# A differential softmax combined by one VectorE instruction in place of two on GpSimd, and three PSUM banks used in turn by transposes, PV products and norm statistics

## The chip, the cores and the metric

The kernel runs on one core of one Trainium2 chip. The metric is the device time of one execution in microseconds: 3506.85 us before (median of three runs, 3505.14 to 3511.03). The engines are TensorE (PE; its weight loads are PEld), VectorE (DVE), ScalarE (ACT), GpSimd (POOL) and SyncE (SP, which here only starts DMA transfers). Each works through its own instructions in the order of the program and waits at an instruction whose inputs or buffers are not ready.

## The reference

Two layers of a diffusion transformer over 128 context tokens and 1024 latent tokens with 1024 features. In each layer a normalised input is projected once to the queries, keys and values of three groups of heads: A (neighbourhood attention, 4 heads), B (windowed attention with a sink, 8 query heads) and C (differential attention, 4 heads); then an output projection with a gated residual, another normalisation and a gated MLP with a convolution over positions. The change is in C:

```
def diff_attn(q, k, v, lam, subln_g, lam_init):
    o1 = dense_attn(q[..., 0, :], k[..., 0, :], v).astype(F32)
    o2 = dense_attn(q[..., 1, :], k[..., 1, :], v).astype(F32)
    o = rmsnorm(o1 - lam * o2, subln_g) * (1.0 - lam_init)
    return o.astype(v.dtype)
```

Each of the two `dense_attn` is softmax(q k / sqrt(d)) v. For the latent tokens the keys are the 1024 latent keys and 256 cached ones, so a block of 128 queries has 128 x 1280 scores per component; the 128 context tokens see only each other.

## The kernel before, in words

Activations lie transposed, features on the 128 partitions and tokens along the free dimension, 1156 columns in three chunks of about 386. A weight matmul is made of three fp32r products of high and low parts (`gemm`, L496). A layer runs as: input projections and attention A and B, woven together after `PLAN`; attention C (`attnC`); the output projection of A and B (`outproj_part`, whose operand is read back from DRAM as `oraw` and split into `o`, L639 and L640); that of C with the normalisation; the MLP (`ffn`, `down`). In layer 0 some modulation vectors are computed between the parts of the output projection (`mod_piece`, L392); those of layer 1 come from `mod_vec` beside the MLP.

`attnC` goes head by head. It loads queries and keys (L699, L703, issued on GpSimd's queue) and the cached keys (`kc`, L705, on SyncE's queue), which GpSimd splits into the key tile (`kr`, L707, L708). There are two buffers for queries and two for keys, one for each component, so a head's loads begin when the last scores of the head before are done. Then come the context block and four pairs of query blocks. For each block and component: score matmuls (L732), a VectorE reduction that copies the scores to `P` and takes the row maximum (L734), an exponential with row sums on ScalarE (L685). With the two row sums in `ss`, VectorE takes the reciprocal of one (L741) and computes the factor that weighs the second component against the first (L742); GpSimd multiplies the second component's `P` by it (L743) and adds it to the first's (L744). The pair goes to `tpv`: 20 transposes in five groups of four (L652), each copied to SBUF by ScalarE (L654), 20 PV matmuls into one bank (L661) and two copies to `O` (L665). Half heads are rescaled (`rows_over`, L757), and after every second head `subln` normalises.

The scheduler that writes the program (`schedule_with_timeline_sim=True`) decides the order on each engine: it takes instructions in the program's order as a priority, with a cost model of its own, and fills what it takes for idle time with later work. So the output projection of A and B stands between the instructions of `attnC`.

PSUM has eight banks, given out by tag. `s` (three) holds scores, `mm` (two) matmul outputs, `tb` (two) transposes and a few others, `pv` (one) PV products. A request for a tag takes the next bank of that tag in turn and waits until the use before it has been released. Input projections go round all eight (`MM_IN`), and statistics of the normalisations take `tb`, `tb` and `pv`.

Of the kernel before, what the change touches and what calls it, by code (L numbers as in the profile page):

```python
# [11 lines left out]
ALU = mybir.AluOpType  # L12
# [23 lines left out]
FGROUP = 3  # L36
NFG = 7
XW = 1156
BANKS = {"s": 3, "tb": 2, "pv": 1, "mm": 2}
MM_FILL = ["mm"]  # L40
MM_SOLO = ["mm", "s", "s", "mm", "s"]
MM_IN = ["mm", "s", "s", "mm", "s", "tb", "tb", "pv"]
ENG = {"v": lambda nc: nc.vector, "p": lambda nc: nc.gpsimd}
FLUSH = (2, 4, 6, 7)
CG = 2
# [3 lines left out]
GATE = 3  # L49
TAGS = {"F": MM_FILL, "P": ["mm", "s", "s", "mm", "s"], "Q": MM_IN}  # L50
MV0 = 12
# [20 lines left out]
def bcast(ap, n):  # L72
    return bass.AP(tensor=ap.tensor, offset=ap.offset, ap=[list(ap.ap[0])] + n)
# [15 lines left out]
class Trunk:  # L89
# [11 lines left out]
    def bank(self, tag):  # L101
        return self.psp.tile([128, 512], F32, name=tag, bufs=BANKS[tag])

# [10 lines left out]
    def run(self):  # L114
        nc, a = self.nc, self.a
        with ExitStack() as st:
# [8 lines left out]
            x = xp.tile([128, KT, XW], F32, name="x")  # L125
# [22 lines left out]
                        st.enter_context(self.tc.issue_after(dm[3].ins))  # L148
            self.gate = dm[GATE]
            self.consts()  # L150
            stats = [self.bank(x) for x in ("tb", "tb", "pv")]
            for t in range(3):
                self.stats(np_, x, stats[t], t, range(KT))
            hp0, hs0 = self.open("h0")
# [6 lines left out]
            for l in range(self.depth):  # L161
# [5 lines left out]
                xs.close()  # L167
                self.mmtags = MM_IN
                self.O = {}
# [27 lines left out]
                x = xp.tile([128, KT, XW], F32, name="x")  # L197
# [19 lines left out]
                np_, ns = self.open("norm", "right")  # L217
                ohp, ohs = self.open("ohl")
                self.h = [None] * 3
                stats = [self.bank(x) for x in ("tb", "tb", "pv")]  # L220
                ow = [self.finO(ohp, t, {k: self.O[k][:, OCHUNK[t][0]:OCHUNK[t][1]] for k in (6, 7)}, 12) for t in range(3)]
                for ts in ((0,), (1, 2)):
                    for ob in range(KT):
                        if ob % 4 == 0:
                            whl = self.wload(a["woc"][l, ob // 4], nc.vector)
                        for t in ts:
                            c0, c1 = OCHUNK[t]
                            ps = self.mm()
# [14 lines left out]
                ms.close()  # L243
                hs1.close()
                if l + 1 < self.depth:
                    stats = [self.bank(x) for x in ("tb", "tb", "pv")]
                    self.op, os_ = self.open("O32")
                    h0n, h0s = self.open("h0")
                    np_, ns = self.open("norm")
                    self.h = [None] * 3  # L250
# [153 lines left out]
    def mod_vec(self, l, j, mp):  # L404
        nc = self.nc
        X = 512 // CG
        acc = [mp.tile([128, X], F32, name="macc", bufs=MODF[1]) for _ in range(2)]
        for k in range(8):
            raw = mp.tile([128, 512], F32, name="mraw", bufs=MODF[0])
            nc.sync.dma_start(raw, self.a["wmv"][12 * l + j - MV0, k])  # L410
            for b in range(CG):
                for v in range(2):
                    c = self.svm[:, CG * k + b, v:v + 1]
                    r = raw[:, X * b:X * b + X]
                    if k == 0 and b == 0:
                        nc.vector.tensor_scalar(acc[v], r, c, None, op0=ALU.mult)
                    else:
                        nc.vector.scalar_tensor_tensor(acc[v], r, c, acc[v], op0=ALU.mult, op1=ALU.add)
        ps = self.bank("pv")
        for i in range(4 // CG):  # L420
            for v in range(2):
                o = 2 * i + v
                nc.tensor.matmul(ps[:, o:8:8 // CG], acc[v][:, 128 * i:128 * i + 128], self.blk, start=True, stop=True)
        self.mod_end(l, j, ps)
# [219 lines left out]
    def tpv(self, ap, items, V, bufs, outs):  # L644
        nc = self.nc
        pts = []
        for g in range(0, len(items), 4):
            its = items[g:g + 4]
            n = 128 * len(its)
            t = self.tb()  # L650
            for j, it in enumerate(its):
                nc.tensor.transpose(t[:, 128 * j:128 * j + 128], it[0], self.ident)  # L652
            pt = ap.tile([128, 512], F32, name="pt", bufs=bufs)
            nc.scalar.activation(pt[:, :n], t[:, :n], AF.Copy)  # L654
            pts.append(pt)
        ps = self.bank("pv")
        left = [sum(it[2] == i for it in items) for i in range(2)]
        first = [True, True]
        for g, (_, vb, i) in enumerate(items):
            left[i] -= 1  # L660
            nc.tensor.matmul(ps[64 * i:64 * i + 64, :128], V[:, vb], pts[g // 4][:, 128 * (g % 4):128 * (g % 4) + 128],  # L661
                             start=first[i], stop=left[i] == 0)
            first[i] = False
        for dst, p0, p1, view in outs:
            nc.scalar.activation(dst, view(ps[p0:p1, :128]), AF.Copy)  # L665
# [21 lines left out]
    def attnC(self, ap):  # L687
        nc, l = self.nc, self.l
        G, qkv = GROUPS["C"], self.qkv["C"]
        lam = self.lam[l]  # L690
        O = V = None
        for h in range(4):
            blk, rw = h // 2, 64 * (h % 2)
            Q, K = [], []
            for c in range(2):
                q = ap.tile([128, W], F32R, name="q", bufs=NQ_C)
                s = qkv[G["q"][blk]][rw // 32 + c]
# [3 lines left out]
                s = qkv[G["k"][blk]][rw // 32 + c]  # L701
# [16 lines left out]
            for q0 in (None, 0, 2, 4, 6):  # L718
                Pq = []
                for i in range(1 if q0 is None else 2):  # L720
                    P2 = []
                    nm = ap.tile([128, 6], F32, name="nm", bufs=4)
                    ss = ap.tile([128, 3], F32, name="ss", bufs=4)
                    qo = C0 if q0 is None else L0 + 128 * (q0 + i)
                    P2 = [ap.tile([128, 1280], F32, name="P", bufs=NP_C) for c in range(2)]
                    parts = [(C0, 0, 128)] if q0 is None else [(L0, 0, 512), (L0 + 512, 512, 512), (L0 + 1024, 1024, 256)]
                    n = parts[-1][1] + parts[-1][2]
                    prev = [self.big] * 2
                    for u, (ko, po, w) in enumerate(parts):
                        for c in range(2):  # L730
                            s = self.sc()[:, :w]
                            nc.tensor.matmul(s, Q[c][:, qo:qo + 128], K[c][:, ko:ko + w], start=True, stop=True)  # L732
                            acc = nm[:, 3 * c + u:3 * c + u + 1]
                            nc.vector.tensor_tensor_reduce(P2[c][:, po:po + w], s, bcast(self.zero, [[0, w]]), -1.0, prev[c],  # L734
                                                           op0=ALU.add, op1=ALU.min, accum_out=acc)
                            prev[c] = acc
                    for c in range(2):
                        self.softrow(P2[c], n, prev[c], ss[:, c:c + 1])
                    r = sums[:, q0 + i:q0 + i + 1] if q0 is not None else ss[:, 2:3]
                    nc.vector.reciprocal(r, ss[:, 0:1])  # L740
                    nc.vector.reciprocal(ss[:, 1:2], ss[:, 1:2])  # L741
                    nc.vector.scalar_tensor_tensor(ss[:, 1:2], ss[:, 1:2], lam[:, 1:2], ss[:, 0:1], op0=ALU.mult, op1=ALU.mult)  # L742
                    nc.gpsimd.tensor_scalar(P2[1][:, :n], P2[1][:, :n], ss[:, 1:2], 0.0, op0=ALU.mult, op1=ALU.add)  # L743
                    nc.gpsimd.tensor_tensor(P2[0][:, :n], P2[0][:, :n], P2[1][:, :n], op=ALU.add)  # L744
                    if q0 is None:
                        nc.vector.tensor_scalar(P2[0][:, :n], P2[0][:, :n], r, None, op0=ALU.mult)
                    Pq.append(P2[0])
                if q0 is None:
                    self.tpv(ap, [(Pq[0][:, :128], 0, 0)], V, NT_C, [(O[rows, C0:C0 + SEQ], 0, 64, lambda z: z)])
                    continue  # L750
                qo = L0 + 128 * q0
                self.tpv(ap, [(Pq[i][:, 128 * k:128 * k + 128], k + 1, i) for k in range(10) for i in range(2)], V, NT_C,
                         [(O[rows, qo + 128 * i:qo + 128 * i + 128], 64 * i, 64 * i + 64, lambda z: z) for i in range(2)])
                if q0 in (2, 6):
                    R = self.rows_over(sums[:, q0 - 2:q0 + 2], 1)[rows]
                    oo = O[rows, L0 + 128 * (q0 - 2):L0 + 128 * (q0 + 2)]
                    nc.vector.tensor_tensor(oo, oo, R, op=ALU.mult)  # L757
                    if h % 2 == 1:
                        for c0, c1 in NCHUNK[:1] if q0 == 2 else NCHUNK[1:]:
                            self.subln(ap, O, c0, c1)  # L760
# [367 lines left out]
```

## Time and profile before

| what | value |
|---|---|
| time, median of three runs | 3506.85 us |
| time of the profiled execution | 3506.57 us |
| its span | 3504.8 us |
| TensorE busy | 3322.5 us (95%) |
| VectorE busy | 2043.1 us (58%) |
| ScalarE busy | 1505.4 us (43%) |
| GpSimd busy | 1213.5 us (35%) |
| instructions | 54130 |

Busy time is a share of the whole span and hides that the stages differ: TensorE is at 88 of 88 us in most stretches of the MLP, and at 70 to 87 in those of attention C. The profiler's granted clock is the share of TensorE's full 2.4 GHz; its lower level, 1.2 GHz, is 0.50. A group of instructions is named by line, engine, operation and tile, with `x` for its count, busy time and the mean of one in ns.

### The profile page before, as it was taken

What the parts mean: (1) busy time and instruction counts of PE and PEld (TensorE: products, weight loads), DVE (VectorE), ACT (ScalarE), POOL (GpSimd) and SP (SyncE); (2) the same over time, 40 slices, a digit from 0 to 9 for tenths busy, and PEclk for the clock granted to TensorE, in tenths of its full rate; (3) what the DMA queues carried; (4) which work ended last, traced back from release to release, by engine and by line L of the source; (5) the groups of instructions that cost most, each with busy time, mean ns of one, the idle gap of its engine ahead of it and who ended that gap; (6) DMA issues with size and microseconds to landing.
All of it is one profiled execution on the core that took longest, in us unless ns stands there. A gap on an engine that the chain in (4) does not pass through costs nothing. (4 is left out here: it accounts for less than half of the span.)

```text
span 3504.8 us, 54130 instructions
## 1 busy us (share of the span) xinstructions
PE 3322.5 (95%) x20398; PEld 3012.4 (86%) x20398; DVE 2043.1 (58%) x4666; ACT 1505.4 (43%) x2905; POOL 1213.5 (35%) x1252
## 2 busy tenths in 40 slices
PE   6999998897899999999999989989888999999999
PEld 4987885684699999999989878858667999999999
DVE  5355466665676765676573554567667544544445
ACT  4566575545432222222245656665564322232222
POOL 6444246645611111111154442476565111111110
PEclk9999998897899999999999999999989999999999
DMA  5764338413112222222136652363201011111112
GB/s 202 203 162 130 94 100 217 133 37 93 34 61 73 85 76 67 82 85 78 43 125 189 169 134 74 109 165 82 52 17 36 32 46 44 43 37 46 46 40 93
DMA packets 184565, 318.21 MB, mean 91 GB/s; under 512 B 58544, under 2 KB 126528, under 8 KB 183920
## 3 DMA queue, kind: packets, MB, share of 16 engines
q1 hardware_dynamic: 170320, 266.18, 24.7%
q0 software_dynamic: 13984, 48.57, 6.8%
q8 instruction: 162, 2.65, 0.3%
q14 instruction: 99, 0.81, 0.1%
HBM read 260.15 MB, written 58.73 MB: 91 GB/s over the span
## 5 line engine op out<-in xcount | busy, mean ns | idle before, releaser
L496 PE MATMUL mm<-h,whl 128*128 128x386 f32 (+2 forms) x4488 | 888.0, 345 | 9.8 <-DVE h L484 4.3
L496 PEld LDWEIGHTS mm<-h,whl 128*128 128x128 f32 x4488 | 796.4, 190 | 29.3 <-DVE h L484 5.8
L496 PE MATMUL s<-h,whl 128*128 128x386 f32 (+2 forms) x4152 | 781.9, 342 | 15.7 <-ACT h L483 10.6
L496 PEld LDWEIGHTS s<-h,whl 128*128 128x128 f32 x4152 | 740.2, 190 | 29.9 <-ACT h L483 15.3
L378 POOL TENSOR_TENSOR whl<-wraw,whl 128x1024 fp32r<-128x1024 f32 x88 | 211.5, 2403 | 1344.5 <-ACT whl L377 1258.2
L685 ACT ACTIVATE P<-P,nm 128x641 f32<-128x641 f32 (+5 forms) x360 | 345.3, 960 | 169.5 <-DVE nm L734 89.6
L377 ACT ACTIVATE whl<-wraw 128x1024 fp32r<-128x1024 f32 (+1 forms) x210 | 207.5, 988 | 450.0 <-PE s L496 255.9
L496 PE MATMUL s<-ah,whl 128*128 128x384 f32 (+1 forms) x1268 | 356.6, 341 | 1.6 <-DVE x L918 1.2
L654 ACT ACTIVATE pt<-tb 128x512 f32<-128x512 f32 (+2 forms) x456 | 237.0, 541 | 147.2 <-PE tb L652 144.1
L652 PE MATMUL tb<-ident,P 128*128 128x128 f32 x1600 | 269.8, 289 | 14.9 <-ACT pt L654 7.5
L661 PE MATMUL pv<-pt,v 128*64 128x128 f32 x3200 | 264.0, 287 | 6.6 <-ACT pt L654 2.9
L918 DVE SCALAR_TENSOR_TENSOR x<-s,m,x 128x128 f32<-128x128 f32 (+3 forms) x347 | 170.0, 514 | 153.6 <-PE s L496 153.2
L918 DVE SCALAR_TENSOR_TENSOR x<-mm,m,x 128x128 f32<-128x128 f32 (+3 forms) x357 | 175.2, 513 | 142.1 <-PE mm L496 141.7
L652 PEld LDWEIGHTS tb<-ident,P 128*128 128x128 f32 x1600 | 189.7, 145 | 72.9 <-issue 36.3
L496 PE MATMUL mm<-ah,whl 128*128 128x384 f32 (+1 forms) x844 | 244.1, 340 | 1.4 <-DVE x L918 1.4
L661 PEld LDWEIGHTS pv<-pt,v 128*64 128x64 f32 x3200 | 173.7, 138 | 83.3 <-issue 54.6
L496 PEld LDWEIGHTS s<-ah,whl 128*128 128x128 f32 x1268 | 233.6, 189 | 5.9 <-DVE x L918 1.7
L496 PE MATMUL mm<-o,whl 128*128 128x384 f32 (+1 forms) x972 | 210.4, 354 | 11.7 <-ACT o L639 6.6
L496 PE MATMUL s<-al,whl 128*128 128x384 f32 (+1 forms) x634 | 215.1, 339 | 0.0
L496 PEld LDWEIGHTS mm<-o,whl 128*128 128x128 f32 x972 | 178.2, 197 | 24.5 <-issue 7.4
L682 PE MATMUL s<-k,q 128*128 128x256 f32 (+2 forms) x816 | 178.5, 333 | 19.2 <-DMA q<-d 11.5
L744 POOL TENSOR_TENSOR P<-P 128x1280 f32<-128x1280 f32 (+1 forms) x72 | 192.2, 2671 | 4.5
(208 smaller groups left out, 4971.8 us busy)
## 6 DMA issues: line engine op xcount, KB each, us to landing
wraw<-wup SPq DMA_DIRECT2D x88, 512.0 KB
mraw<-wmod SPq DMA_DIRECT2D x48, 512.0 KB
mraw<-wmv SPq DMA_DIRECT2D x96, 256.0 KB
wraw<-wdn SPq DMA_DIRECT2D x64, 384.0 KB
k<-d POOLq DMA_DIRECT2D x80, 288.5 KB, 6.5
wraw<-win SPq DMA_DIRECT2D x36, 512.0 KB
d<-hl SPq DMA_DIRECT2D x28, 386.0 KB
q<-d POOLq DMA_DIRECT2D x32, 289.0 KB, 6.6
```

What stands on the lines that cost most here:

```text
L377: nc.scalar.activation(hl[:, 0, :n], raw[:, :n], AF.Copy)
L378: lo_eng.tensor_tensor(hl[:, 1, :n], raw[:, :n], hl[:, 0, :n].bitcast(F32), op=ALU.subtract)
L496: nc.tensor.matmul(ps, w_, r_[:, a:b], start=(i == 0), stop=(i == tot - 1))
L652: nc.tensor.transpose(t[:, 128 * j:128 * j + 128], it[0], self.ident)
L654: nc.scalar.activation(pt[:, :n], t[:, :n], AF.Copy)
L661: nc.tensor.matmul(ps[64 * i:64 * i + 64, :128], V[:, vb], pts[g // 4][:, 128 * (g % 4):128 * (g % 4) + 128], start=first[i], stop=left[i] ...
L682: nc.tensor.matmul(dst, q, view(ks[i]), start=(i == 0), stop=(i == 1))
L685: self.nc.scalar.activation(P[:, :n], P[:, :n], AF.Exp, scale=-1.0, bias=nm, accum_out=sums)
L744: nc.gpsimd.tensor_tensor(P2[0][:, :n], P2[0][:, :n], P2[1][:, :n], op=ALU.add)
L918: nc.vector.scalar_tensor_tensor(xx, ps[:, s - a:e - a], m[:, col + ob, v:v + 1], xx, op0=ALU.mult, op1=ALU.add)
```

## The change

In `attnC` the two GpSimd instructions L743 and L744 become one VectorE instruction that multiplies the second component by the factor and adds the first. The factor itself (L742) is computed by another form with the same three inputs. The bank tags become `s` (three), `tb` (three) and `mm` (two): PV products, the vectors of `mod_vec` and the third bank of the statistics are taken from `tb`, in turn with the transposes. Lines after the combine have a number smaller by one in the changed kernel.

```
-BANKS = {"s": 3, "tb": 2, "pv": 1, "mm": 2}
+BANKS = {"s": 3, "tb": 3, "mm": 2}
...
-MM_IN = ["mm", "s", "s", "mm", "s", "tb", "tb", "pv"]
+MM_IN = ["mm", "s", "s", "mm", "s", "tb", "tb", "tb"]
...
-            stats = [self.bank(x) for x in ("tb", "tb", "pv")]
+            stats = [self.bank(x) for x in ("tb", "tb", "tb")]
...
-        ps = self.bank("pv")
+        ps = self.tb()
...
-                    nc.vector.scalar_tensor_tensor(ss[:, 1:2], ss[:, 1:2], lam[:, 1:2], ss[:, 0:1], op0=ALU.mult, op1=ALU.mult)
-                    nc.gpsimd.tensor_scalar(P2[1][:, :n], P2[1][:, :n], ss[:, 1:2], 0.0, op0=ALU.mult, op1=ALU.add)
-                    nc.gpsimd.tensor_tensor(P2[0][:, :n], P2[0][:, :n], P2[1][:, :n], op=ALU.add)
+                    nc.vector.tensor_scalar(ss[:, 1:2], ss[:, 1:2], ss[:, 0:1], lam[:, 1:2], op0=ALU.mult, op1=ALU.mult)
+                    nc.vector.scalar_tensor_tensor(P2[0][:, :n], P2[1][:, :n], ss[:, 1:2], P2[0][:, :n], op0=ALU.mult, op1=ALU.add)
```

The statistics' line stands three times in `run`, the `ps` line once in `mod_vec` and once in `tpv`.

The scheduler writes a new order. On GpSimd, at the change from the first to the second head of C in layer 0, there stood before (`q<-d` and `k<-d` are the loads of queries and keys, `kr<-kc` needs the load of cached keys):

```order
L699 DMA q<-d_12_5669 32x1156 x4
L703 DMA k<-d_14_5612 64x1154 x2
L708 TENSOR_TENSOR k<-kc,kr 128x256
L640 TENSOR_TENSOR o<-oraw,o 128x384
L743 TENSOR_SCALAR P<-P,ss 128x1280
L699 DMA q<-d_12_5669 32x1156 x4
L703 DMA k<-d_14_5612 64x1154 x2
L743 TENSOR_SCALAR P<-P,ss 128x1280
L707 TENSOR_SCALAR kr<-kc,hsel 128x256
L744 TENSOR_TENSOR P<-P 128x1280
L640 TENSOR_TENSOR o<-oraw,o 128x384 x2
L744 TENSOR_TENSOR P<-P 128x1280
```

and stands now:

```order
L640 TENSOR_TENSOR o<-oraw,o 128x386 x2
L640 TENSOR_TENSOR o<-oraw,o 128x384 x4
L640 TENSOR_TENSOR o<-oraw,o 128x386 x4
L640 TENSOR_TENSOR o<-oraw,o 128x384 x2
L699 DMA q<-d_12_5669 32x1156 x4
L703 DMA k<-d_14_5612 64x1154 x2
L708 TENSOR_TENSOR k<-kc,kr 128x256
L699 DMA q<-d_12_5669 32x1156 x4
L703 DMA k<-d_14_5612 64x1154 x2
L707 TENSOR_SCALAR kr<-kc,hsel 128x256
L708 TENSOR_TENSOR k<-kc,kr 128x256
```

The combines of the last two blocks are gone from between the loads and `kr<-kc`, and twelve splits of the projection's operand now stand ahead of the loads. On TensorE at the same place there stood before (`s<-k,q 128x128` is the context block of the next head, `mm<-o,whl` the output projection):

```order
L661 MATMUL pv<-pt,v 64x128 x12
L732 MATMUL s<-k,q 128x128
L496 MATMUL mm<-o,whl 128x384 x3
L496 MATMUL mm<-o,whl 128x386 x6
L496 MATMUL mm<-o,whl 128x384 x7
L732 MATMUL s<-k,q 128x128
L732 MATMUL s<-k,q 128x512 x4
L732 MATMUL s<-k,q 128x256
L652 MATMUL tb<-ident,P 128x128 x2
L496 MATMUL mm<-o,whl 128x384 x10
L496 MATMUL mm<-o,whl 128x386 x6
L652 MATMUL tb<-ident,P 128x128 x6
```

and stands now, between the first and the second score of the context block:

```order
L652 MATMUL tb<-ident,P 128x128 x9
L496 MATMUL mm<-o,whl 128x384 x6
L496 MATMUL mm<-o,whl 128x386
L652 MATMUL tb<-ident,P 128x128 x4
L496 MATMUL mm<-o,whl 128x386 x5
L652 MATMUL tb<-ident,P 128x128 x4
L661 MATMUL tb<-pt,v 64x128 x16
L673 MATMUL tb<-ident,sums 128x128 x4
L496 MATMUL mm<-o,whl 128x384 x5
L661 MATMUL tb<-pt,v 64x128 x4
L496 MATMUL mm<-o,whl 128x384 x6
L732 MATMUL s<-k,q 128x128
```

The last pair's transposes and PV products have moved from behind the next head's scores to ahead of its second component. On TensorE at the start of the third head of C in layer 1 there stands before:

```order
L732 MATMUL s<-k,q 128x128
L732 MATMUL s<-k,q 128x512 x2
L496 MATMUL mm<-o,whl 128x386 x12
L652 MATMUL tb<-ident,P 128x128 x6
L496 MATMUL mm<-o,whl 128x384 x4
L732 MATMUL s<-k,q 128x512
L496 MATMUL mm<-o,whl 128x384 x3
L732 MATMUL s<-k,q 128x512
```

and now:

```order
L732 MATMUL s<-k,q 128x128
L732 MATMUL s<-k,q 128x512 x3
L767 MATMUL tb<-sq,ones_86 128x384
L732 MATMUL s<-k,q 128x512
L732 MATMUL s<-k,q 128x256 x2
L767 MATMUL tb<-sq,ones_86 128x386
L732 MATMUL s<-k,q 128x512 x4
L652 MATMUL tb<-ident,P 128x128
```

The output projection, whose 432 matmuls stood in the second and third head there, now stands in the first and second.

## Rows read from the trace of the kernel before

**Rows 1.** Stretches of attention C: busy time of each engine, clock, DMA share
```profile
537.00:897.00 360.00, 308.80 (x1950) 219.73 (x1950) 212.78 (x628) 186.15 (x343) 205.98 (x168) 0.87 0.40 113
...
2300.00:2610.00 310.00, 266.43 (x1780) 207.33 (x1776) 206.00 (x620) 179.80 (x338) 201.24 (x159) 0.91 0.27 72
```

**Rows 2.** Stretches by head and gap; columns: us, PE, PEld, DVE, ACT, POOL, clock, DMA
```profile
537.00:602.00 65.00, 57.98 (x387) 35.90 (x386) 47.94 (x143) 44.55 (x86) 46.63 (x50) 0.87 0.71 222
602.00:622.00 20.00, 7.95 (x25) 5.92 (x21) 3.10 (x10) 2.45 (x8) 10.75 (x9) 0.59 0.72 157
...
690.00:700.00 10.00, 4.28 (x15) 1.32 (x14) 1.85 (x2) 1.99 (x4) 5.47 (x6) 0.71 1.17 248
...
820.00:866.00 46.00, 40.77 (x252) 25.58 (x250) 37.43 (x125) 32.33 (x57) 26.75 (x15) 0.87 0.04 9
...
2300.00:2350.00 50.00, 41.40 (x303) 27.17 (x299) 39.49 (x141) 38.98 (x80) 35.74 (x32) 0.96 0.45 150
2350.00:2372.00 22.00, 15.67 (x96) 12.41 (x96) 8.62 (x27) 9.25 (x21) 18.44 (x21) 0.77 0.79 171
2372.00:2435.00 63.00, 63.00 (x447) 54.42 (x447) 49.08 (x147) 40.68 (x73) 47.78 (x37) 1.00 0.29 74
...
2450.00:2518.00 68.00, 64.27 (x422) 54.39 (x420) 50.76 (x144) 35.33 (x61) 29.17 (x16) 0.97 0.09 29
...
2535.00:2585.00 50.00, 42.91 (x273) 28.90 (x272) 39.98 (x122) 36.12 (x62) 33.35 (x19) 0.84 0.04 9
```

**Rows 3.** Groups by line and shape, 535 to 900 us: GpSimd's combine, copies of PV
```profile
L744 POOL TENSOR_TENSOR P<-P 128x1280 f32<-128x1280 f32 x32 | 94.9, 2968 | 1.9
...
L743 POOL TENSOR_SCALAR P<-P,ss 128x1280 f32<-128x1280 f32 x32 | 43.4, 1356 | 68.1 <-DVE ss L742 34.2 <-ACT pt L654 14.8 <-PE s L732 10.2
...
L665 ACT ACTIVATE O<-pv 64x128 f32<-64x128 f32 x36 | 9.8, 272 | 25.3 <-PE pv L661 25.0
```

**Rows 4.** Timeline of GpSimd at a head change; columns: start, duration, engine, instruction, wait
```profile
599.50 2.04 POOL L699 DMA_DIRECT2D q<-d  x4
...
609.68 0.48 POOL L707 TENSOR_SCALAR kr<-kc,hsel 128x256 fp32r<-128x256 f32 x1 [5.46 <-DMA kc<-kc]
...
613.81 1.97 POOL L640 TENSOR_TENSOR o<-oraw,o 128x384 fp32r<-128x384 f32 x2 [0.80 <-ACT o L639]
615.73 2.90 POOL L744 TENSOR_TENSOR P<-P 128x1280 f32<-128x1280 f32 x1
```

**Rows 5.** Timeline of TensorE: projection matmuls, weight loads of PV and transposes
```profile
713.08 3.96 PE L496 MATMUL mm<-o,whl 128*128 128x384 f32 x21
...
732.76 0.85 PEld L661 LDWEIGHTS pv<-pt,v 128*64 128x64 f32 x16 [0.17 <-issue]
...
875.98 0.64 PEld L652 LDWEIGHTS tb<-ident,P 128*128 128x128 f32 x6 [0.77 <-POOL P L744]
```

**Rows 6.** Timeline at the end of attention C, layer 0
```profile
866.97 2.90 POOL L744 TENSOR_TENSOR P<-P 128x1280 f32<-128x1280 f32 x1
867.10 1.35 ACT L685 ACTIVATE P<-P,nm 128x1280 f32<-128x1280 f32 x1
867.71 2.58 DVE L770 SCALAR_TENSOR_TENSOR O<-O,pp,oy 128x386 f32<-128x386 f32 x1
...
873.03 2.90 POOL L744 TENSOR_TENSOR P<-P 128x1280 f32<-128x1280 f32 x1
```

**Rows 7.** VectorE: line L526 (min/median/max in ns), and the reductions by shape, 535 to 900 us
```profile
L526 DVE SCALAR_TENSOR_TENSOR qg<-t,qg x78: 546/559/1080, 81.6 to 2306.8; 128x386 f32<-128x386 f32 x52, 128x384 f32<-128x384 f32 x26
...
L734 DVE CUSTOM_DVE_ANT_0 P<-s,zero,nm 128x512 f32<-128x512 f32 x64 | 46.9, 745 | 8.1 <-PE s L732 7.1
L734 DVE CUSTOM_DVE_ANT_0 P<-s,zero,nm 128x256 f32<-128x256 f32 x64 | 30.2, 477 | 11.7 <-PE s L732 11.3
```

**Rows 8.** VectorE's factor L742: the whole program, and 820 to 866 us
```profile
L742 DVE SCALAR_TENSOR_TENSOR ss<-ss,lam x72: 205/219/2727, 547.2 to 2582.9; 128x1 f32<-128x1 f32 x72
...
L742 DVE SCALAR_TENSOR_TENSOR ss<-ss,lam 128x1 f32<-128x1 f32 x8 | 5.5, 692 | 0.0
```

More of the change, by code (lines that the diff above doesn't have):

```diff
@@ L219, in run @@
                 self.h = [None] * 3
-                stats = [self.bank(x) for x in ("tb", "tb", "pv")]
+                stats = [self.bank(x) for x in ("tb", "tb", "tb")]
                 ow = [self.finO(ohp, t, {k: self.O[k][:, OCHUNK[t][0]:OCHUNK[t][1]] for k in (6, 7)}, 12) for t in range(3)]
@@ L245, in run @@
                 if l + 1 < self.depth:
-                    stats = [self.bank(x) for x in ("tb", "tb", "pv")]
+                    stats = [self.bank(x) for x in ("tb", "tb", "tb")]
                     self.op, os_ = self.open("O32")
@@ L655, in tpv @@
             pts.append(pt)
-        ps = self.bank("pv")
+        ps = self.tb()
         left = [sum(it[2] == i for it in items) for i in range(2)]
```

## The prediction

> **What bounds the kernel now.** I read the views by stretch first, then the groups of the differential-attention sections by line, then the timelines of two places in them. TensorE is the bound nearly everywhere. The stretches in which it is not full are the two sections where differential attention (C) runs beside the output projection of A and B: 537 to 897 us in layer 0 and 2300 to 2610 us in layer 1. There TensorE is busy for 308.8 of 360 us at a granted clock of 0.87 and for 266.4 of 310 us at 0.91 [rows 1]. The combine is only in these sections, and the feed-forward stages keep their instructions, so what the change can move is a part of 51 + 44 us of idle time and of the slow clock.
>
> Inside a section four heads follow each other [rows 2]. Where TensorE has projection matmuls between a head's own work it is full or nearly so (63.0 of 63 us, 64.3 of 68). Where it has none, VectorE sets the pace: 37.4 of 46 us busy in the last head of layer 0 and 40.0 of 50 in that of layer 1, at clocks of 0.87 and 0.84. Between heads there is a gap (602 to 622 us: TensorE 8.0 busy of 20), in which keys and queries of the next head are loaded.
>
> **The change part by part.** *Combine off GpSimd.* Two instructions per block of 128 queries go: 1.36 and 2.97 us, 32 of each of this size per layer [rows 3]. GpSimd is busy for 206.0 of the 360 us, so its load as such is not the bound [rows 1]; its order is. At a head change the multiplications of the finished blocks stand ahead of `kr<-kc` (L707) and their additions behind it. L707 waits for a load until 609.68 us, so the last addition runs at 615.73, and the 20 transposes and 20 PV calls of the pair come after the gap rather than in it [rows 4]. The new instruction has no such load ahead of it, and the order of the change puts these transposes ahead of the next head's second score. Their price on TensorE is 20 x 0.64/6 + 40 x 0.85/16 = 4.2 us (a PV call is two records) [rows 5]. It is a gain only where TensorE is full afterwards and the gap has idle time for it: both changes inside layer 0's first three heads (12.0 and 5.7 us idle) and the first of layer 1 (6.3) [rows 2], 3 x 4.2 = 12.6 us.
>
> *The tail of a section.* The last exponential ends at 868.45 us; the addition that follows from it begins at 873.03 and the transposes that need it at 875.98 [rows 5, 6]. In the change a reciprocal and a factor come first (some 0.4 us, L742's median twice [rows 8]), then the new instruction (1.5), so transposes near 870.5: 5.5 us gained. Nothing lies beside this end: normalisation and the last projection wait for it. Layer 1 has the same pattern: 11 us together.
>
> *Combine on VectorE.* The trace has no instruction of this kind with 1280 elements. From below: one with 386 elements takes 0.56 us. From above: three reductions that cover 1280 columns take 2 x 0.745 + 0.477 = 1.97 us. I take 0.56 + 894 x (0.745 - 0.477)/256 = 1.50 us, the 386-element row, nearest in kind, with the slope of the reductions [rows 7]. VectorE gets 32 x 1.50 = 48 us per layer. It gets back what the small instruction L742 waits today: its median is 0.22 us, its longest 2.73, and in the last head of layer 0 eight take 5.5 us, 3.7 over their medians [rows 8]. In heads with projection work this lies beside a full TensorE. In a head without it is on the path: six of eight blocks' instructions (two fall into the gap or the tail), 9.0 us, less 3.7, and of the rest about half in VectorE's idle time (8.6 of 46 us [rows 2]): 3 us a head. The ends of the duration, over 18 such instructions in three heads, are -17 and +8 us.
>
> *The order of TensorE.* A cost may come from here. In the order of before the projection matmuls stand at 10, 167, 255 and 0 in the four heads of layer 0 and at 7, 212, 213 and 0 in layer 1; in the order of the change at 102, 210, 120, 0 and at 132, 300, 0, 0. One takes 3.96/21 = 0.189 us [rows 5]. Layer 0: the first head gets 92 x 0.189 = 17.4 us into 7.0 of idle, +10.4; the second +8.1; the third loses 25.5; the fourth +3. Sum -4. (Six modulation matmuls pass from the fourth to the third and cancel.) Layer 1: the first gets 23.6 us into 8.6 of idle, +15; the second 88 x 0.189, +16.6; the third has no projection left, so VectorE paces it as it paces the fourth today, 50 + 3 = 53 us for 68, -15; the fourth +3. Sum +19.6.
>
> *GpSimd's queue.* In the order of the change the first 12 subtractions of the projection's operand (L640) stand ahead of the next head's query loads. Before, the fifth waited until 613.81 us, and query loads went out at 599.50 [rows 4]. If that load still comes so late, the query loads go 14 us later; but it now stands ahead of the cache load on SyncE's queue, not behind it. Bounds 0 to +14 us a layer; I take 0, since TensorE has projection work queued there.
>
> *Banks.* A PV call used to have a bank of its own; now every third bank of transposes waits for the copies of the PV before it, two of 0.27 us [rows 3]: at worst 2 x 20 calls x 0.54 = +22 us in the C sections. On the other side PV stands in 302 rows of TensorE's order, not 368, and a change of kind costs a pause of 0.17 us [rows 5]: 66 x 0.17 = 11 us over the program. I take -3, the C sections' share by calls (40 of 152). Elsewhere input projections lie beside it. The statistics had three banks and have three.
>
> Sum: -12.6 - 11 - 4 + 19.6 - 3 = -11 us. Against the profiled execution (3506.6 us, 1.8 over its span and 0.3 below the median of three) that is **3495 us**.
>
> One rule speaks against the gain on VectorE. L770, an instruction with two operands in SBUF and 386 elements, took 2.58 us while GpSimd's addition of 866.97 us ran [rows 6], and one of the same kind and size takes 0.56 [rows 7]. The Trainium skill (GPSIMD Engine Reference, Specifications) says that GpSimd shares its SBUF interfaces with VectorE, with contention where a VectorE instruction has two SBUF inputs. The trace agrees, and by that the new instruction can be held as well. Outside the combine GpSimd is busy for 206 - 138 = 68 of 360 us [rows 1, 3], so of 32 instructions some 6 would meet something of about 1 us: 6 us a layer on VectorE at most, a third of it on the path, and a sum of 3499.
>
> **Rivals.** *VectorE becomes the bound (slower).* In no head without projection work is it over 40.0/50 = 80% busy [rows 2]. If 80% is what this mix of waits allows, the heads of layer 1 hold 179.4 + 26 x 1.50 - 8 = 210 us of VectorE work, 263 us at 80% for 231 today: +32. Its head change then gives nothing, and with tails and layer 0's order it is +32 - 11 - 4 = +17: **3524 us**. For it: no head shows more. Against: 8.6 and 10 us of those heads are waits that more queued work would fill. It decides from the point where VectorE is at 80% over a whole head with projection work.
>
> *The loads go out late:* GpSimd's queue costs its upper bound, +28: **3523**. For it: the order; against: SyncE's new order.
>
> *No net change:* the gaps are as long as their loads and the pair's transposes are hidden there anyway: -11 - 4 + 19.6 - 3 = +1.5: **3508**. For it: in the gaps TensorE waits for loads.
>
> *More gain:* heads without projection run at VectorE's sum, (4 x 0.745 + 2 x 0.477 + 0.3 + 1.5) x 8 = 46 us rather than 53, in three heads: -21 more, **3474**. For it: L742's stretches and slow scores make up the idle time there.
>
> **How the numbers follow.** Forecast 0.40, more gain 0.22, VectorE 0.15, late loads 0.10, no net change 0.13. A measurement of this kernel can tell about 0.2%, 7 us, from no change. Faster: 0.40 x 0.85 + 0.22 = 0.56; same: 0.40 x 0.12 + 0.13 x 0.8 + 0.10 x 0.3 = 0.18; slower the rest, 0.26. The range leaves out the far parts of the slower rivals and of the gain: 3468 to 3526; the forecast's own is 3484 to 3507.
>
> **What would show it.** Right: the two GpSimd groups gone, a VectorE group of 64 at 1.4 to 1.6 us, L742 near 0.2; the last transposes of a section 2 to 3 us behind the last exponential; transposes inside the gap at a head change; the third head of layer 1 near 53 us at a low clock, and its first and second longer than now. Wrong: TensorE waiting for reductions in heads with projection work; query loads that leave long after a head's last score; transposes that wait for the PV copies; a change of over 10 us outside the two sections.

## The result and the profile after

The changed kernel takes 3538.89 us (median of four runs, 3537.42 to 3540.90) beside 3508.59 us for the kernel before, a ratio of 1.0087 with a 95% interval of 1.0070 to 1.0105: 30 us slower, where 3495 was forecast. The profiled execution spans 3538.9 us against 3504.8. TensorE's busy time is the same, 3322.5 us before and 3322.4 in the changed kernel's page, so the 34 us are idle time of TensorE:

```profile
PE 3322.4 (94%) x20398; PEld 3022.8 (85%) x20398; DVE 2100.2 (59%) x4738; ACT 1509.9 (43%) x2905; POOL 941.9 (27%) x1108
```

Nearly all of it arises between the input projection and the end of attention C. Stretches in us, from the first score matmul of each head; "start" counts from the begin of the span (layer 0) or from the last matmul of layer 0's MLP (layer 1), "tail" from the last exponential's begin to C's output projection:

| | start of C | head 1 | head 2 | head 3 | head 4 | tail |
|---|---|---|---|---|---|---|
| layer 0 before | 535.6 | 70.4 | 101.6 | 108.9 | 50.7 | 23.3 |
| layer 0 after | 556.9 | 91.0 | 96.0 | 77.3 | 52.5 | 18.6 |
| layer 1 before | 494.1 | 55.2 | 82.5 | 87.6 | 53.8 | 22.8 |
| layer 1 after | 509.6 | 89.7 | 94.0 | 59.6 | 57.2 | 17.1 |

C starts 21.3 and 15.5 us later, its first heads are 20.6 and 34.5 us longer, its third heads 31.6 and 28.0 us shorter. Added up, the rows of layer 0 grow by only 1.8 us (890.5 to 892.3) and those of layer 1 by 31.2 (796.0 to 827.2): the loss is nearly all in layer 1. The changed kernel's busy times by the same stretches show what the late time is made of (columns as in [rows 2]):

```profile
521.00:556.90 35.90, 27.65 (x236) 22.33 (x234) 15.34 (x45) 20.95 (x47) 18.47 (x30) 0.92 0.63 128
556.90:647.90 91.00, 66.09 (x422) 47.16 (x422) 61.00 (x171) 41.65 (x77) 26.57 (x35) 0.82 0.63 193
...
744.00:821.20 77.20, 71.46 (x498) 52.53 (x497) 58.75 (x166) 41.72 (x76) 11.14 (x17) 1.00 0.41 116
821.20:875.00 53.80, 45.76 (x295) 31.18 (x293) 45.47 (x139) 37.19 (x67) 2.52 (x3) 0.81 0.12 23
...
2319.40:2409.10 89.70, 63.35 (x405) 51.30 (x405) 62.97 (x174) 41.07 (x76) 27.65 (x36) 0.79 0.44 131
...
2503.10:2562.70 59.60, 47.15 (x304) 32.14 (x302) 48.81 (x145) 39.73 (x73) 10.97 (x18) 0.81 0.28 55
2562.70:2621.20 58.50, 50.94 (x292) 36.00 (x293) 45.76 (x139) 36.25 (x65) 2.53 (x3) 0.72 0.09 19
```

Before, the first two of these stretches of layer 0, and the first head of layer 1, read:

```profile
521.00:535.60 14.60, 14.60 (x142) 12.09 (x141) 9.74 (x33) 9.49 (x24) 7.69 (x14) 1.00 1.06 198
535.60:606.00 70.40, 59.58 (x401) 36.95 (x398) 48.92 (x148) 46.17 (x91) 49.88 (x54) 0.88 0.74 221
...
2300.90:2356.20 55.30, 46.70 (x349) 31.02 (x345) 39.02 (x140) 42.12 (x84) 41.88 (x41) 0.94 0.54 162
```

From 521 us to C's first score TensorE used to be full (14.60 of 14.60 us); now it idles for 8.3 us there, and the first head idles for 24.9 us rather than 10.8, at a lower clock (0.82 for 0.88). In layer 1 the first head idles for 26.4 us rather than 8.6, at 0.79 rather than 0.94. Of the 21.3 and 15.5 us by which C starts later, 11.7 and 6.8 are idle time of TensorE; in the rest it does transposes and PV products of A and B that used to run beside C's first head. What TensorE waits for is in the changed kernel's waits, layer 0 and then layer 1 (total, times, longest; the 7.9 us for queries end at the first score of C, the others lie in the first head):

```profile
PE s L732 <- POOL k L708: 10.1, 1, 10.1
PE s L732 <- DMA q<-d: 7.9, 1, 7.9
PE s L732 <- DVE nm L734: 4.3, 1, 4.3
PE mm L392 <- DMA mraw<-wmod: 3.5, 1, 3.5
...
PE s L732 <- POOL k L708: 11.7, 1, 11.7
PE s L732 <- DMA k<-d: 5.9, 1, 5.9
PE s L732 <- DVE nm L734: 4.7, 3, 4.4
PE mm L496 <- ACT o L639: 4.7, 2, 3.3
```

The longest wait is for the split of the second component's cached keys (L708). The timeline of the changed kernel in layer 1 shows why it is late:

```profile
2323.22 3.89 SPq L296 DMA_DIRECT2D x<-xsp  x3
...
2327.20 3.65 SPq L839 DMA_DIRECT2D odr<-O  x1
...
2331.60 1.34 SPq L705 DMA_DIRECT2D kc<-kc  x1
...
2340.24 0.20 POOL L628 MEMSET O<- 128x1 f32 x4 [10.62 <-DMA odr<-O]
2344.43 0.48 POOL L707 TENSOR_SCALAR kr<-kc,hsel 128x256 fp32r<-128x256 f32 x1 [3.99 <-DMA kc<-kc]
...
2345.77 2.66 PE L732 MATMUL s<-k,q 128*128 128x256 f32 x5 [11.68 <-POOL k L708]
```

On SyncE's queue the 128 KB of cached keys now stand behind three loads of x (1536 to 1544 KB each) and a store; in the order of before they stood ahead of them. On GpSimd the zeros of O's border (L628) stand ahead of the split and wait for the same store.

What was done to the combine itself shows in VectorE's groups of the changed kernel:

```profile
L743 DVE SCALAR_TENSOR_TENSOR P<-P,ss 128x1280 f32<-128x1280 f32 x64 | 100.0, 1562 | 0.7
...
L742 DVE TENSOR_SCALAR ss<-ss,lam 128x1 f32<-128x1 f32 x72 | 19.4, 270 | 0.7
...
L769 DVE SCALAR_TENSOR_TENSOR O<-O,pp,oy 128x386 f32<-128x386 f32 x8 | 4.9, 614 | 0.0
```

1.56 us each, and GpSimd's groups [rows 3] are gone. VectorE's busy time grew by 57 us (2043.1 to 2100.2), not by the 103 of the new instructions. The end of layer 0's section, the changed kernel's timeline, which answers to the end of before:

```profile
873.71 1.35 ACT L685 ACTIVATE P<-P,nm 128x1280 f32<-128x1280 f32 x1
...
875.69 1.55 DVE L743 SCALAR_TENSOR_TENSOR P<-P,ss 128x1280 f32<-128x1280 f32 x1
...
877.30 3.17 PE L652 MATMUL tb<-ident,P 128*128 128x128 f32 x17 [1.19 <-DVE P L743]
```

The transposes begin 2.2 us behind the last exponential's end; before, they began 7.5 us behind it [rows 6].

### The profile page after: what moved, and what is told of

Same layout as the page of the kernel before. It is cut to its first block, busy times and chain, and to the rows that moved or that the text cites. A ratio compares the mean times of both kernels' runs of the same rounds, so it can differ in the third digit from the quotient of the medians.

```text
span 3538.9 us, 53953 instructions
## 1 busy us (share of the span) xinstructions
PE 3322.4 (94%) x20398; PEld 3022.8 (85%) x20398; DVE 2100.2 (59%) x4738; ACT 1509.9 (43%) x2905; POOL 941.9 (27%) x1108
## 5 line engine op out<-in xcount | busy, mean ns | idle before, releaser
L496 PE MATMUL mm<-h,whl 128*128 128x386 f32 (+2 forms) x4488 | 897.3, 346 | 7.5 <-DVE h L484 4.3
L496 PEld LDWEIGHTS mm<-h,whl 128*128 128x128 f32 x4488 | 794.7, 190 | 26.4 <-DVE h L484 5.8
L496 PE MATMUL s<-h,whl 128*128 128x386 f32 (+2 forms) x4152 | 781.7, 343 | 18.8 <-ACT h L483 12.2
L496 PEld LDWEIGHTS s<-h,whl 128*128 128x128 f32 x4152 | 738.4, 190 | 35.9 <-ACT h L483 17.5
L685 ACT ACTIVATE P<-P,nm 128x641 f32<-128x641 f32 (+4 forms) x360 | 345.7, 961 | 212.9 <-DVE nm L734 120.4
L496 PE MATMUL s<-ah,whl 128*128 128x384 f32 (+1 forms) x1268 | 356.9, 342 | 1.5 <-DVE x L917 1.2
L661 PE MATMUL tb<-pt,v 128*64 128x128 f32 x3200 | 251.3, 287 | 4.1 <-ACT pt L654 4.1
L496 PE MATMUL mm<-ah,whl 128*128 128x384 f32 (+1 forms) x844 | 244.4, 341 | 1.4 <-DVE x L917 1.4
L496 PEld LDWEIGHTS s<-ah,whl 128*128 128x128 f32 x1268 | 233.8, 189 | 5.8 <-DVE x L917 1.7
L661 PEld LDWEIGHTS tb<-pt,v 128*64 128x64 f32 x3200 | 176.4, 140 | 72.4 <-issue 44.2
L732 PE MATMUL s<-k,q 128*128 128x512 f32 (+2 forms) x400 | 162.4, 464 | 63.3 <-POOL k L708 21.8
L496 PE MATMUL s<-al,whl 128*128 128x384 f32 (+1 forms) x634 | 215.3, 340 | 0.0
L496 PE MATMUL mm<-o,whl 128*128 128x384 f32 (+1 forms) x972 | 205.1, 350 | 6.1 <-ACT o L639 4.7
L962 ACT ACTIVATE ah<-yv 128x384 fp32r<-128x384 f32 x132 | 69.4, 526 | 278.8 <-DVE yv L960 278.8
```

Of the source, the lines that this page charges most:

```text
L496: nc.tensor.matmul(ps, w_, r_[:, a:b], start=(i == 0), stop=(i == tot - 1))
L685: self.nc.scalar.activation(P[:, :n], P[:, :n], AF.Exp, scale=-1.0, bias=nm, accum_out=sums)
L962: nc.scalar.activation(ah[:, o:o + n], y, AF.Copy)
```

## The experiments

Each was timed beside the kernel before on the same chip, whose median was 3510 to 3514 us in these sessions; the changed kernel itself was timed beside 3508.59 alone.

**The two halves of the change apart.** The first has only the new combine:

```
-                    nc.vector.scalar_tensor_tensor(ss[:, 1:2], ss[:, 1:2], lam[:, 1:2], ss[:, 0:1], op0=ALU.mult, op1=ALU.mult)
-                    nc.gpsimd.tensor_scalar(P2[1][:, :n], P2[1][:, :n], ss[:, 1:2], 0.0, op0=ALU.mult, op1=ALU.add)
-                    nc.gpsimd.tensor_tensor(P2[0][:, :n], P2[0][:, :n], P2[1][:, :n], op=ALU.add)
+                    nc.vector.tensor_scalar(ss[:, 1:2], ss[:, 1:2], ss[:, 0:1], lam[:, 1:2], op0=ALU.mult, op1=ALU.mult)
+                    nc.vector.scalar_tensor_tensor(P2[0][:, :n], P2[1][:, :n], ss[:, 1:2], P2[0][:, :n], op0=ALU.mult, op1=ALU.add)
```

> The kernel before with the combine as one VectorE instruction and the banks left as they were (transposes two, PV one). Theory O (the loss comes from the order that the shared banks bring about: C's keys and cached keys arrive late, TensorE idles in the first head of C): no loss here, the tails of the two sections give 10 us, 3485 to 3500 us, first head of C near 70 and 55 us long as before. Theory V (VectorE became the bound through the combine): slower than before, 3525 to 3540 us.

3474.05 us, ratio 0.9903 (0.9887 to 0.9919): 34 to 37 us faster than before, and 11 us below what theory O said. It beats both kernels and was not beaten by any other that was run. Its profiled execution took 3483.18 us, 9 us more than its median, so its stretches show less than the whole gain. The second has only the banks:

```
-BANKS = {"s": 3, "tb": 2, "pv": 1, "mm": 2}
+BANKS = {"s": 3, "tb": 3, "mm": 2}
```

(and the uses of `pv` as in the change.)

> The changed kernel with the combine put back on GpSimd in its two instructions, the banks as changed. Theory O: the whole loss is here and the gain of the combine is missing, 3543 to 3560 us, first head of C near 90 us in both layers. Theory V: as before, 3503 to 3513 us.

3522.84 us, ratio 1.0036 (1.0022 to 1.0050), slower, but less than expected. So the banks are what costs, theory V falls, and theory O holds in kind, though both times lie below its ranges. The parts don't add up: -37 and +12 make -25, together they make +30. C's start and its first heads are late and long with the banks alone (552.7 us; heads of 81.6 and 87.1 us) and not with the combine alone (538.9; 75.3 and 58.7).

**Where the banks act.** The combine on VectorE, with three banks in turn in one part of the program only. `turn` is set around attention C, or around the input projection and attention A and B:

```
+    def tb(self):
+        if not self.turn:
+            return self.bank("tb")
+        self.nturn += 1
+        return self.bank(("tb", "tb", "pv")[self.nturn % 3])
```

> The combine on VectorE, three banks in turn for transposes and PV inside attention C alone; attention A and B, the input projection and the rest keep the banks of before. Theory O (the loss arises in the order of attention A and B): like the combine alone, 3483 to 3500 us. Theory P (in C the transposes wait for the copies of the PV that shares their banks): over the combine alone by 10 to 22 us, 3498 to 3520 us.

3487.75 us, ratio 0.9940 (0.9926 to 0.9954): 14 us over the combine alone, first heads 73.7 and 64.1 us. The time lies in theory O's range, but it is not that of the combine alone.

> The combine on VectorE, three banks in turn for transposes, PV and the input projection in attention A and B alone; in C the banks of before. Theory O (the loss arises in the order of attention A and B): most of the distance between the combine alone and the changed kernel is here, 3510 to 3530 us. Theory P (it arises where C's transposes wait for the PV that shares their banks): near the combine alone, 3472 to 3485 us.

3510.46 us, ratio 1.0004 (0.9994 to 1.0013): 36 us over the combine alone. More than half of the 65 us between the combine alone and the changed kernel comes from the banks of the input projection and attention A and B, though C's own banks are those of before. It is not lost where these banks are used: TensorE's idle time up to C's first score is 37.0 and 21.9 us in the two layers, where the combine alone has 41.3 and 22.6. It is lost in the first head of layer 1, here and in the combine alone (columns as in [rows 2]):

```profile
2293.60:2384.40 90.80, 63.06 (x377) 49.32 (x378) 63.93 (x174) 41.86 (x77) 24.94 (x35) 0.79 0.45 129
```

```profile
2284.10:2342.80 58.70, 48.31 (x367) 33.95 (x366) 50.64 (x153) 44.26 (x87) 19.55 (x26) 0.97 0.51 155
```

TensorE idles for 27.7 us rather than 10.4. So here it is the order that these banks bring about that costs, and not a wait at a bank. The two layers of this kernel differ, and that is a comparison inside one run: in layer 0 the order left the cached keys ahead of x and 25 projection matmuls in the first head, in layer 1 it put them behind x, with 132. The waits of this kernel in the first heads, layer 1 (90.8 us long) and layer 0 (71.7):

```profile
PE s L742 <- POOL k L718: 14.2, 1, 14.2
PE s L742 <- DMA k<-d: 10.6, 2, 5.4
...
PE s L742 <- issue: 3.7, 1, 3.7
```

In C the rival P had a price of 10 to 22 us, and the 14 us fit it in size. But TensorE waits for the copies of PV (L665) only 1.5 and 1.4 us in the changed kernel's two sections, and 1.1 and 2.0 us in the kernel with the turn in C alone, where the combine alone has no such wait: 3 of the 14 us are where P puts them. Whether the order makes up the rest was not settled.

**The waits of the first head.** First the late cached keys alone, in the changed kernel:

```
-                nc.sync.dma_start(raw, self.a["kc"][l, :, 6 + 2 * h + c])
+                nc.gpsimd.dma_start(raw, self.a["kc"][l, :, 6 + 2 * h + c])
...
-                O = self.newO(OT["C"] + h // 2)
+                O = self.op.tile([128, W], F32, name="O", bufs=2)
...
+                if q0 == 6 and h % 2 == 0:
+                    for c in (0, L0 - 1, L0 + T, L0 + T + 1):
+                        nc.gpsimd.memset(O[:, c:c + 1], 0.0)
```

> The changed kernel with the cached keys loaded on GpSimd's queue rather than SyncE's, where they stood behind the loads of x, and with the zeros of O's border columns written later, so that neither stands before the cached keys' split. TensorE's order is the same to a few instructions. Theory L (the wait of the first head for its second component's cached keys, 10.1 and 11.7 us, is the loss): these waits go, 3514 to 3522 us. Theory Q (the order of TensorE alone, with late queries and keys, is the loss; the wait is only where it shows): 3533 to 3541 us, the time lost again at the next wait.

3533.96 us, ratio 1.0068 (1.0055 to 1.0080): 5 us, and its interval overlaps that of the changed kernel. The wait was there, and taking it away gave nearly nothing. It was replaced at once, in the waits of this kernel's first heads, layer 0 and layer 1:

```profile
PE mm L392 <- DMA mraw<-wmod: 12.4, 1, 12.4
...
PE mm L496 <- ACT o L639: 13.6, 3, 13.2
```

These are the matmuls that fill TensorE's order in the first head (modulation, L392, and projection, L496). They stand between C's scores, their operands are loaded only from C's start on, behind x, and TensorE, which works in order, stops at them: the first heads idle for 26.1 and 25.1 us, about as in the changed kernel. So the next kernel holds back the filling work instead, and leaves the cached keys where they were:

```
+                    if h == 0 and q0 == 4 and i == 0:
+                        self.hold = e.ins
...
+                with self.tc.issue_after(self.hold):
+                    if l == 0:
+                        for j in (4, 5):
+                            self.mod_piece(l, j, ab, self.mm(), NMC)
+                    self.outproj_part(x, ab, 0, 2, a["woa"][l])
```

> The changed kernel, in which the loads for the first part of the output projection and the first modulation vectors go out only after the exponential of the fifth block of C's first head, so that the order holds 48 and 54 projection matmuls in that head rather than 102 and 132. Theory S (two waits stand side by side in the first head, that for the cached keys and that of filling matmuls whose operands come late; either is hidden behind the other): with one of them left 3525 to 3537 us. Theory F (filling matmuls in the first head are the loss by themselves): 3505 to 3520 us. Theory K (the start of C is late and the work is only moved): 3535 to 3545 us.

3535.53 us, ratio 1.0073 (1.0058 to 1.0088): 3 us, and these intervals overlap as well. Now the cached keys are the long wait again, in this kernel's first heads 9.8 us and 8.0:

```profile
PE s L733 <- POOL k L709: 9.8, 1, 9.8
...
PE s L733 <- POOL k L709: 8.0, 1, 8.0
```

And both edits in one kernel:

> The changed kernel with both: cached keys loaded on GpSimd's queue with O's border zeros written later, and the filling work held back as in the run beside it. Theory S: both waits of the first head go, some 20 us of it in each layer less what the later heads take for the projection that they now hold, 3505 to 3520 us. Theory K: no more than the late loads alone gave, 3528 to 3540 us.

3492.93 us, ratio 0.9952 (0.9937 to 0.9967): 46 us less than the changed kernel, where the single edits gave 5 and 3. The gain is larger than theory S said, and S holds in layer 1 alone. The longest waits that are left in the first heads, layer 0 and layer 1:

```profile
PE mm L393 <- DMA mraw<-wmod: 12.4, 1, 12.4
...
PE s L737 <- DMA k<-d: 5.6, 2, 3.0
...
PE s L737 <- POOL k L709: 3.6, 1, 3.6
```

In layer 1 both waits are gone but for 3.6 us: the first head takes 65.7 us for 89.7 and idles for 15.9 us, where the changed kernel had 26.4 and the single edits 25.1 and 28.8, so either wait did hide the other there. In layer 0 the modulation's load took the place of the cached keys, and the first head idles for 24.7 us as before the edits. The head is shorter all the same, 79.7 us for 91.0, since the order now holds 32 projection matmuls in either first head, fewer than with the holding back alone (48 and 54). C's start is 8 us earlier in layer 0 and 9 in layer 1. So the two waits explain some 10 of the 46 us; the rest comes with a new order in both layers and was not taken apart.

**Are these edits good by themselves?** The same two on the combine alone, and on the kernel before:

> The combine alone (banks of before) with the two edits that freed the first head of the changed kernel: cached keys on GpSimd's queue with O's zeros later, and the filling work's loads held back. Theory S (those edits answer to waits that only the order of the shared banks makes): no gain, within 8 us of the combine alone, 3468 to 3484 us. Theory G (they are a gain to any version): 3430 to 3460 us.

3498.51 us, ratio 0.9964 (0.9952 to 0.9976): 24 us worse than the combine alone.

> The kernel before with the same two edits and nothing else. Theory S: near the kernel before, 3500 to 3515 us. Theory G: 3460 to 3485 us.

3488.85 us, ratio 0.9934 (0.9921 to 0.9948): 22 us better than before. Neither theory: the edits change the order everywhere, and what they bring depends on the order that they meet. One at a time on the combine alone:

> The combine alone with only the filling work's loads held back, cached keys on SyncE's queue as before. Theory H1 (it was the holding back that cost 24 us on top of the combine alone, since modulation and projection then lack cover in the third head of layer 0): near 3495 to 3502 us. Theory H2 (it was the cached keys' new queue): 3470 to 3480 us.

3498.02 us, ratio 0.9959 (0.9944 to 0.9974).

> The combine alone with only the cached keys on GpSimd's queue and O's zeros written later. Theory H1: 3468 to 3480 us. Theory H2: 3490 to 3502 us.

3487.78 us, ratio 0.9930 (0.9913 to 0.9947). Holding back costs the whole 24 us (H1 on that point), but the other edit costs 14 by itself, which H1 did not say. In all three the third head of layer 0 grew, from 98.9 us to 106.9, 111.3 and 108.9, and the modulation's matmuls wait there for their loads for 9.4, 8.8 and 10.5 us rather than 4.7.

**VectorE's price.** A second combine, of no use to anyone, behind each of the 64:

```
+                    if q0 is not None:
+                        nc.vector.scalar_tensor_tensor(P2[1][:, :n], P2[1][:, :n], ss[:, 1:2], P2[0][:, :n], op0=ALU.mult, op1=ALU.add)
```

> The combine alone on VectorE (banks of before), with a second instruction of the same kind and size behind each of the 64, whose result nobody uses: 64 times 1.6 us more on VectorE. Theory V (VectorE is the bound of attention C): nearly all of it is paid, 3555 to 3575 us. Theory H (only heads without projection work pay, 18 to 22 of the 64, and a part of it hides in VectorE's idle time there): 3490 to 3510 us.

3524.32 us, ratio 1.0043 (1.0029 to 1.0057): 50 us over the combine alone for 101 us of VectorE, between the two theories. The last heads without projection work, in the combine alone (first fence) and with it twice (columns as in [rows 2]):

```profile
798.00:852.40 54.40, 47.14 (x289) 29.88 (x288) 45.69 (x139) 36.82 (x66) 1.63 (x2) 0.82 0.03 8
2507.00:2562.40 55.40, 47.47 (x288) 30.04 (x288) 46.03 (x139) 37.12 (x67) 2.52 (x3) 0.82 0.14 26
```

```profile
799.00:864.60 65.60, 54.16 (x294) 34.98 (x294) 56.90 (x148) 37.62 (x67) 3.47 (x3) 0.71 0.10 20
2534.00:2597.20 63.20, 51.54 (x303) 32.10 (x303) 56.95 (x148) 38.01 (x67) 3.32 (x4) 0.81 0.11 22
```

There 11.2 and 10.9 us more of VectorE cost 11.2 and 7.8 us: such a head pays most of it. In the first of the two the clock is lower as well, 0.71 for 0.82, and how much of the 11.2 us that is was not measured. VectorE is at 84 and 83% in the combine alone, at 87 and 90% with two. The rest of the 50 us lies in heads with projection work, whose order changed too (60 and 66 projection matmuls in the first heads for 25 and 26), so it isn't VectorE's price alone.

## Why the prediction was wrong, point by point

**The step that failed is "Banks".** It took -3 us for C and said of the rest: "Elsewhere input projections lie beside it." Measured, the banks cost 65 us on top of the new combine and 12 on top of the old one. The new bank split changes the order of the input projection and attention A and B, which I had not compared; I read only the sections of C in it. In the trace the last matmul of the input projection before C ends 16.0 us later in layer 0 (523.2 to 539.2) and 15.4 later in layer 1, and between it and C's first score stand 88 matmul records where there were 126 and 140. The loads of C's first queries and keys leave GpSimd's queue within 3 us of that projection's end, in layer 0 before (first fence) and in the changed kernel:

```profile
520.60 2.01 POOL L699 DMA_DIRECT2D q<-d  x4
```

```profile
539.56 2.00 POOL L699 DMA_DIRECT2D q<-d  x4
```

They leave 19.0 us later, and 16.4 later in layer 1, and the attention work that covered them has been done before. But C's later start is only in part a loss: of its 36.8 us 18.5 are idle time, and layer 0 as a whole loses 1.8 us. The larger loss is the first head of C in layer 1, 34.5 us longer with 17.7 more of idle time: there the order holds 132 projection matmuls for 7 and has the cached keys behind x. The kernel with these banks in A and B alone shows the same head, 90.8 us. A term that was bounded for waits at a bank was not bounded for what the scheduler makes of a bank.

**Heads of C: the sum near, the parts not.** Head changes and TensorE's order together were to cost 19.6 - 4 - 12.6 = +3 us. The four heads took -14.8 us in layer 0 (331.6 to 316.8) and +21.4 in layer 1 (279.1 to 300.5), +6.6. But the first heads grew by 20.6 and 34.5 us where 10.4 and 15 stood, the second changed by -5.6 and +11.5 where +8.1 and +16.6 stood, and the third shrank by 31.6 and 28.0 where 25.5 and 15 stood. The third head of layer 1, forecast at 53 us, took 59.6. I priced filling matmuls by their time on TensorE and forgot that their operands must be there: 0.189 us a matmul holds where the operand has come, and in the first head the order has them wait for `o` and for the modulation's weights.

**The tails: right.** 11 us forecast; 23.3 to 18.6 and 22.8 to 17.1, 10.4 together.

**The combine on VectorE: right.** 1.50 us estimated, 1.56 measured. Heads without projection were to be 3 us longer: 1.8 and 3.4. The pay-back was there: L742 took 34.4 us in 72 instructions and takes 19.4; the eight instructions of 386 elements that were L770 took 12.3 us and take 4.9. The contention that the prediction feared for the new instruction did not hold it: its median is 1.548 us, its longest 1.908.

**GpSimd's queue: right that it costs nothing, with a cost elsewhere.** At the head change of layer 0 the query loads leave at 636.51 us, 0.1 us behind the head's last score (636.41), past the twelve splits. The rival "late loads" named the wrong place: the loads that went out late were those at the start of C, queries and keys on GpSimd's queue and cached keys on SyncE's.

**The rival "VectorE becomes the bound"** gave 3524 us and the right sign, for a reason that the runs refute: the combine alone is 35 us faster than before, with VectorE at 84% in heads that it held to 80. The rival "more gain" has the combine alone's 3474 us by luck: it took heads without projection work at 46 us, and they take 54.4 and 55.4.

**The combine's gain was underrated.** Without the banks' term the forecast came to 3498; the combine alone ran at 3474. In layer 0 the second and third heads fell from 101.6 and 108.9 us to 84.8 and 98.9. Before, TensorE waited in these two for the projection's operand (6.6 us) and for modulation weights (15.1); in the combine alone it waits 4.7 for the weights and not for the operand. That the splits of the operand run when they are due because GpSimd's 4.3 us per block [rows 3] are out of the way is not shown: the kernel before with the two edits keeps these 4.3 us, and there too TensorE waits in the same heads for the modulation's weights only 3.0 us and not for the operand. The order may have done it in both. Where the rest of the gap to 3474 comes from was not shown either.

**What stays open:** why the combine gains 37 us on the old banks and loses 16 on the new ones (3522.8 to 3538.9). Of that loss 9.4 us lie in the first head of layer 0, where the order then holds 102 projection matmuls for 78; an order that is held fixed while one instruction changes was not tried.

## What to carry to other kernels

Where a scheduler writes the order, a change of buffers or banks can be a change of order in the whole program, as here: compare the order of every engine in every stage that uses the bank, and look where the last producer of the next stage's input stands. A wait that the profile names may have a second one behind it that costs as much; only taking away both shows it (in the first head of layer 1 idle time of 25.1 and 28.8 us with either gone, 15.9 with both). And where an edit changes the order too, its gain is not the price of the wait that it was made for (46 us for the two edits here, some 10 of them in those waits). A change with two halves is measured in halves first: here one was worth 35 us and the other took back nearly twice that.

## What the runs showed of the hardware

In these kernels a small load was late by what stood ahead of it on its own queue, and less by what was under way on another: in the changed kernel the 128 KB of cached keys took from their issue at 2331.60 us to 2344.43 on SyncE's queue behind 4.6 MB of x and a store of 0.6 MB, 12.8 us. On GpSimd's queue, in the kernel with the late loads away, whose timeline reads

```profile
2316.20 3.44 SPq L296 DMA_DIRECT2D x<-xsp  x3
...
2320.99 0.61 POOL L705 DMA_DIRECT2D kc<-kc  x1
...
2326.43 0.48 POOL L707 TENSOR_SCALAR kr<-kc,hsel 128x256 fp32r<-128x256 f32 x1 [3.14 <-DMA kc<-kc]
```

they were issued at 2320.99 us with the same loads of x under way, and there by 2326.43, 5.4 us. The Trainium skill (DMA: Bandwidth & Descriptors, Issuing engines are not separate DMA queues) says that transfers of all issuing engines run on the same 16 DMA engines and interleave; the 5.4 us agree with that, and the queue is worth 7 us to this load.

VectorE's instructions were shorter with GpSimd's combine gone: its busy time was 46 us under what the new instructions add, of which L742 and L770's line, all sizes, are 15 and 9 us. The banks are not the reason: with the banks alone, and the combine on GpSimd, VectorE is busy for 2061.8 us, in the changed kernel for 2100.2, 38 more where the new instructions are 103. L742 has another form as well, so its 15 us are not GpSimd's alone.
